# Tiles placed at equal addresses modulo 512 bytes, and the first MLP product as three 256-column matmuls

## The chip, the cores and the metric

The kernel runs on one core of one Trainium2 chip. The metric is the device time of one execution in microseconds, taken as the median of several runs. Nothing else runs on the chip.

## The reference

A trunk of four residual sub-layers over 256 tokens of width 2048, all in float32: a gated linear recurrence (RG-LRU), an MLP, dilated attention, and a second MLP, each behind an RMS norm, and a final norm.

```python
for i in range(2):
    h = _rmsnorm(x, mix_norm[i])
    x = x + (_rglru_block(h, ...) if i == 0 else _dilated_attention_block(h, ...))
    x = x + _mlp(_rmsnorm(x, mlp_norm[i]), mlp_w1[i], mlp_w2[i])
return _rmsnorm(x, final_norm)

def _mlp(h, w1, w2):                    # w1 2048 x 8192, w2 8192 x 2048
    u = jnp.einsum('bsd,df->bsf', h, w1)
    u = jnp.square(jax.nn.relu(u))
    return jnp.einsum('bsf,fd->bsd', u, w2)
```

The recurrent block projects to 2 x 2560 columns (`w_in`), runs a convolution, ten block-diagonal gates of width 256 and a scan, and projects back (`w_out`). The attention block projects to q, k and v (`w_qkv`) and back (`w_o`).

## The kernel before, in words

**Number format.** A float32 operand is cut into a high part, rounded to the matmul's float32r format, and a low part, the remainder. A product is the sum of three matmuls: high by high, high by low, low by high. ScalarE cuts the weights' high part `whi` (line 86), VectorE their low part `wlo` (line 90). A tokens' tile holds both parts side by side: columns 0 to 255 are the high part for 256 tokens, columns 256 to 511 the low part. The tokens' tiles are `xT0` to `xT3` (the normed input, four blocks of 128 features in each), `aT0` to `aT19` (a hidden activation, 128 features each) and `chl` (the gates' input).

**Units.** All weights stream in as units of up to 1 MiB (128 partitions by 2048 columns) in one fixed order, the order in which they are used. A unit is 16 blocks of 128 by 128, or 4 of 128 by 512. There are 3 raw buffers, 4 of `whi` and 3 of `wlo`, and loading and cutting run some units ahead. The order of all work is written out by hand: a list of items, one for each unit, with follow-up work hung on items behind (`after(n, ...)`).

**Three forms of product.** All their matmuls are issued from one line, 142.
- `stand_w`: a 128 x 128 block of weights is loaded into the array and 256 columns of a tokens' tile stream past. Three matmuls of 256 columns for each block. Used by the recurrent block's input projection (`acc<-xT,whi` and `acc<-xT,wlo` of 128x256), and written out in the same pattern in the gates (`g<-chl,...`).
- `stand_w2`: the same, but `whi` meets all 512 columns (high and low) in one matmul, which leaves two sums in a 512-column accumulator, and `wlo` meets the 256 high columns. One matmul of 512 and one of 256 for each block. Used by the first MLP product (`w1`): 64 units in each MLP.
- `stand_x`: a 128 x 128 block of tokens is loaded and 512 columns of weights stream past. 24 matmuls of 512 columns a unit. Used by q, k, v (`acc<-whi,xT`, `acc<-wlo,xT`), the output projections and the second MLP product (`acc<-whi,aT`, `acc<-wlo,aT`).

Every matmul has its own weight load (`PEld` in the profile), which the engine runs beside the matmul ahead.

**The first MLP product's end** is `u_done`: VectorE adds the two halves of the accumulator (line 462), multiplies the clipped sum by the norm's factor (line 463), ScalarE squares (465) and rounds (467), and VectorE takes the low part (471). Its result is `aT0` to `aT15`.

**Addresses.** Tiles are placed one behind the other within a partition, in the order in which a pool first meets their names. The byte at which they begin, modulo 512, as the built program has it:

| tile | before |
|---|---|
| raw, whi, wlo (all buffers) | 320 |
| aT0 to aT15 | 320 |
| xT0 to xT3 | 256 |
| chl, aT16 to aT19 | 352 |

A block's 128 columns are 512 bytes and a tokens' half 1024, so every operand that a matmul reads begins at the same place modulo 512 as its tile does. The tile `xb` (two rows of 259 floats, 2072 bytes) stands ahead of `chl` and `aT16` to `aT19` in its pool, and the small tile `rs` behind `xT3`. The accumulators, and the operands of the attention's own small matmuls, stay where they are throughout.

Of the kernel before, what the change touches and what calls it, by code (L numbers as in the profile page):

```python
# [10 lines left out]
F32 = mybir.dt.float32  # L11
F32R = mybir.dt.float32r
AF = mybir.ActivationFunctionType
OP = mybir.AluOpType
AX = mybir.AxisListType

D = 2048
S = 256
NT = S // 128
# [4 lines left out]
DFF = 8192  # L24
# [2 lines left out]
KR = DR // 128  # L27
NCH = D // 512
UW = 2048

PC = {}
_at = 0
# [17 lines left out]
def trunk(ctx: ExitStack, tc: tile.TileContext, a: dict, out: bass.AP):  # L50
    nc = tc.nc
    P = 128

    perm = ctx.enter_context(tc.tile_pool(name="perm", bufs=1))
# [1 line left out]
    psum = ctx.enter_context(tc.tile_pool(name="psum", bufs=1, space=bass.MemoryType.PSUM))  # L56
    ctx.enter_context(tc.manual_schedule())

    # ---- the order of the weights: units of up to 1 MiB, each with its columns a partition
    units = []  # L60

    def unit(ap, width=UW):
        units.append((ap, width))
        return len(units) - 1

    raw, split = {}, {}
    seen = {"load": 0, "hi": 0, "lo": 0}

    def load(i, step=UW):
        ap, width = units[i]  # L70
        r = wts.tile([P, UW], F32, name="raw", bufs=RAW_BUFS)
        raw[i] = []
        for at in range(0, width, step):
            s = slice(at, min(at + step, width))
            raw[i].append((s, r[:, s]))
            nc.sync.dma_start(r[:, s], ap[:, s])

    def new_hi(i):
        split[i] = (wts.tile([P, UW], F32R, name="whi", bufs=HI_BUFS),)

    def new_lo(i):
        split[i] += (wts.tile([P, UW], F32R, name="wlo", bufs=3),)

# [32 lines left out]
    def item(u, fn):  # L116
        items.append((u, fn))
# [18 lines left out]
    lru = Scope()  # L136

    def after(n, fn, *args):
        later.setdefault(now[0] + n, []).append((fn, args))

    def mm(o, l, r, start, stop):
        nc.tensor.matmul(o, l, r, start=start, stop=stop, skip_group_check=True)  # L142

    # ---- constants and small parameters
    par = perm.tile([P, NPAR], F32, name="par")
    con = perm.tile([P, NCON], F32, name="con")
    ident = con[:, 0:128]
# [1 line left out]
    def pcol(name, j):  # L149
        at = PC[name][0] + j  # L150
        return par[:, at:at + 1]

    xc = [perm.tile([P, NT, 512], F32, name=f"xc{n}") for n in range(NCH)]
    ssq = perm.tile([P, NT, NCH], F32, name="ssq", bufs=2)
    state = {}

    def hilo(hi_out, lo_out, src):
# [8 lines left out]
    def xT(k):  # L166
        return state["xT", k // 4][:, k % 4, :]
# [44 lines left out]
        nc.scalar.activation(rb, tr[:, 0, :], AF.Copy)  # L212
        state["rstdB"] = rb

    # ---- products of three parts: the weights' tile stands still, or the tokens' tile does
    def stand_w(ps, u, ks, w_at, first, last):
        hi, lo = split[u]
        for j, k in enumerate(ks):
            x = xT(k)
            s = slice((w_at + j) * 128, (w_at + j + 1) * 128)  # L220
            mm(ps, hi[:, s], x[:, 0:256], first and j == 0, False)
            mm(ps, hi[:, s], x[:, 256:512], False, False)
            mm(ps, lo[:, s], x[:, 0:256], False, last and j == len(ks) - 1)

    def stand_w2(ps, u, ks, w_at, first, last):
        hi, lo = split[u]
        for j, k in enumerate(ks):
            x = xT(k)
            s = slice((w_at + j) * 128, (w_at + j + 1) * 128)
            if first and j == 0:  # L230
                mm(ps, hi[:, s], x, True, False)
                mm(ps[:, 0:256], lo[:, s], x[:, 0:256], False, False)
            else:
                mm(ps[:, 0:256], lo[:, s], x[:, 0:256], False, False)
                mm(ps, hi[:, s], x, False, last and j == len(ks) - 1)

    def stand_x(acc, u, get, ks, first, last, ts=range(NT)):
        hi, lo = split[u]
# [9 lines left out]
    def acc_tile():  # L248
        return psum.tile([P, 512], F32, name="acc", bufs=4)

    accs = {}

    def out_item(key, u, get, ks, first, last, done):
        def run():
            if first:
                accs[key] = [acc_tile() for _ in range(NT)]
            stand_x(accs[key], u, get, ks, first, last)
            if last:
                after(0, done, accs.pop(key))
        item(u, run)  # L260
# [23 lines left out]
    def new_aT(j):  # L284
        t = (perm if j < 16 else lru).tile([P, 512], F32R, name=f"aT{j}")
        state["aT", j] = t
        return t

    # ---- the recurrent block
    spn = perm.tile([P, 2, KR], F32, name="spn")  # L290

    spw = perm.tile([P, 6, KR], F32, name="spw")
# [22 lines left out]
    blk = {}  # L315

    def xb_done(h, j, ps):
        if j == 0:
            blk[h, "xb"] = lru.tile([P, 2, S + 3], F32, name="xb")
            blk[h, "c"] = lru.tile([P, 2, S], F32, name="c", bufs=2)  # L320
            nc.vector.memset(blk[h, "xb"][:, :, 0:3], 0.0)
        xb, c, ch = blk[h, "xb"], blk[h, "c"], 2 * h + j
        nc.vector.tensor_mul(xb[:, j, 3:], ps[:, :S], state["rstdB"])
        nc.vector.tensor_scalar(c[:, j, :], xb[:, j, 3:], pcol("cw", 60 + ch), pcol("cb", ch),
                                op0=OP.mult, op1=OP.add)
        w = lru.tile([P, 2, S], F32, name="a") if h == 1 and j == 0 else None
        for i in range(3):
            if w is not None:
                nc.gpsimd.tensor_scalar(w[:, j, :], xb[:, j, i:i + S], pcol("cw", 20 * i + ch), None, op0=OP.mult)  # L329
                nc.gpsimd.tensor_add(c[:, j, :], c[:, j, :], w[:, j, :])  # L330
            else:
                nc.vector.scalar_tensor_tensor(c[:, j, :], xb[:, j, i:i + S], pcol("cw", 20 * i + ch),
                                               c[:, j, :], op0=OP.mult, op1=OP.add)
        if j == 1:
            after(1, conv_split, h)
# [120 lines left out]
            for kq in range(5):  # L456
                oproj(n, kq)

    # ---- the MLP, DFF in four parts
    def u_done(j, ps):  # L460
        r = lru.tile([P, S], F32, name="mr", bufs=2)
        nc.vector.tensor_reduce(r, ps.rearrange("p (b c) -> p c b", b=2), axis=AX.X, op=OP.add)  # L462
        nc.vector.scalar_tensor_tensor(r, r, 0.0, state["rstdB"], op0=OP.max, op1=OP.mult)  # L463
        uu = lru.tile([P, S], F32, name="mu", bufs=2)
        nc.scalar.activation(uu, r, AF.Square)  # L465
        t = new_aT(j)
        nc.scalar.activation(t[:, 0:256], uu, AF.Copy)  # L467
        after(1, u_low, t, uu)
# [4 lines left out]
    def plan_mlp(w1, w2, done):  # L473
        for c in range(4):
            us = []

            def part(j, ks, first, last, us=us, c=c):
                def run():
                    if first:
                        accs["u", j] = acc_tile()  # L480
                    stand_w2(accs["u", j], us[j], ks, ks[0], first, last)
                    if last:
                        after(1 if c == 0 and j == 0 else 0, u_done, j, accs.pop(("u", j)))
                item(us[j], run)

            us.extend(unit(w1[c * 16 + j]) for j in range(16))
            at = 0
            if c == 0:
                for j in range(2):
                    part(j, range(0, 12), True, False)  # L490
                for j in range(2):
                    part(j, range(12, 16), False, True)
                at = 2
            for j in range(at, 16):
                part(j, range(16), True, True)
            for n in range(NCH):
                last_c = c == 3
                if last_c and n == NCH - 1 and done is final_done:
                    final_items([unit(w2[(c * 4 + n) * 4 + kq]) for kq in range(4)])
                    continue  # L500
                for kq in range(4):
                    u = unit(w2[(c * 4 + n) * 4 + kq])
                    out_item(("m", n), u, aT, range(4 * kq, 4 * kq + 4), kq == 0, kq == 3,
                             done(n) if last_c else (lambda acc, n=n: add_x(n, acc)))

    # ---- dilated attention
    att = {}
    scale = HD ** -0.5

# [92 lines left out]
            for kq in range(4):  # L602
                oproj(n, kq)

    # ---- the end
    def final_done(n):
        def done(acc):
            if n == 0:
# [53 lines left out]
        nc.sync.dma_start(gB, a["g_fin"].to_broadcast([P, D]))  # L662
        state["gB"] = gB

    # ---- the plan
    first = [None] * 4
    lru.open("rec")
    plan_rec()
# [7 lines left out]
    item(None, load_g)  # L676
    plan_mlp(a["w1_1"], a["w2_1"], final_done)

    # ---- the start: the first units by the chunks of the tokens, as both arrive
    nc.sync.dma_start(par, a["par"])  # L680
    warm = perm.tile([P, 1], F32, name="warm")
    nc.vector.memset(warm, 0.0)
# [14 lines left out]
    for n in range(NCH):  # L697
        xg[n] = perm.tile([P, 4, S], F32, name="xg", bufs=2)
        rs = [wts.tile([P, UW], F32, name="raw", bufs=RAW_BUFS) for _ in range(3)] if n == 0 else rs
        for h in range(2 if n == 0 else 1):  # L700
            w = 2 if n == 0 else 4
            nc.sync.dma_start(xg[n][:, h * w:(h + 1) * w, :], a["xT"][:, 4 * n + h * w:4 * n + (h + 1) * w, :])
            for i in range(3):
                if n or i == 0:
                    s = slice(n * 512 + h * w * 128, n * 512 + (h + 1) * w * 128)
                elif h:
                    s = slice(0, 512)
# [5 lines left out]
        for h in range(2 if n == 0 else 1):  # L713
# [6 lines left out]
            for i in range(3):  # L720
# [3 lines left out]
                for at, (s, _) in enumerate(raw[i]):  # L724
                    if s.stop == n * 512 + (h + 1) * w * 128:
# [5 lines left out]
                        ks = range(s.start // 128, s.stop // 128)  # L731
# [14 lines left out]
    for n in range(NCH):  # L746
        s = slice(n * 512, (n + 1) * 512)
        r = xc[n // 2][:, n % 2, :]
# [14 lines left out]
    ps = psum.tile([P, 2, S], F32, name="tr", bufs=2)  # L763
# [102 lines left out]
```

## Time and profile before

| | us |
|---|---|
| runs | 2205.47, 2207.06, 2207.97 |
| median | 2207.06 |
| span of the profiled execution, first to last instruction | 2202.6 |
| TensorE busy with matmuls, in that span | 2179.4 |
| VectorE, ScalarE, GpSimd busy | 1315.3, 1062.0, 80.1 |
| HBM traffic | 411 MB, 187 GB/s over the span |

The profile gives the profiled execution's span; its whole time is not listed apart from the three runs. The median stands 4.5 us above the span, for what lies ahead of the first instruction and behind the last. TensorE's busy share counts overlapping instructions once, and the ends of matmuls are modelled, so the pace of a stream of matmuls is read from their starts. The program's stages by time: start to 43 us, recurrent input projection with gates to 276, `w_out` to 382, first MLP to 1095 (four rounds of 16 units of `w1` and 16 of `w2`), attention to 1484, second MLP to the end.

### The profile page before, as it was taken

How to read it: one execution, taken by the hardware profiler on the slowest of the kernel's cores; microseconds unless marked ns; L12 is line 12 of the kernel's file. 1: busy time of each engine (PE TensorE's matmuls, PEld its weight loads, DVE VectorE, ACT ScalarE, POOL GpSimd, SP SyncE). 2: the span in 40 equal slices, each digit the busy share in tenths (PEclk: the TensorE clock that was granted, in tenths of full speed). 3: DMA queues.
4: the chain of work that ended last, by engine and by line, in shares of the span. 5: the costliest groups of instructions: out<-in, count | busy, mean ns of one | idle time of the engine just before them, and what ended most of it. 6: DMA issues, size and time to landing. Idle time of an engine off the chain costs nothing.

```text
span 2202.6 us, 27925 instructions
## 1 busy us (share of the span) xinstructions
PE 2179.4 (99%) x11722; PEld 1877.8 (85%) x11722; DVE 1315.3 (60%) x1392; ACT 1062.0 (48%) x1163; POOL 80.1 (4%) x42
## 2 busy tenths in 40 slices
PE   7999999999999999999999999999999999999998
PEld 7999988888888888888888888888888888888886
DVE  8899855654564564565455555456545645645654
ACT  5787755543443443344445445455434434433442
POOL 2221100000000000000000000000000000000001
PEclk9999999999999999999999999999999999999999
DMA  6666555555555555555554455455555555555553
GB/s 222 207 211 205 197 191 191 180 196 196 176 192 197 184 190 193 189 191 191 182 191 162 163 177 177 162 199 183 195 196 177 191 196 184 190 193 190 191 191 115
DMA packets 61694, 413.30 MB, mean 188 GB/s; under 512 B 6784, under 2 KB 7168, under 8 KB 13440
## 3 DMA queue, kind: packets, MB, share of 16 engines
q1 hardware_dynamic: 61568, 411.51, 54.7%
q8 instruction: 92, 1.51, 0.3%
q14 instruction: 34, 0.28, 0.0%
HBM read 409.39 MB, written 2.10 MB: 187 GB/s over the span
## 4 chain that ended last, share of the span: by engine, by line
PE 96%; DVE 2%; ACT 1%; POOL 0%; issue 0%; DMA 0%; SPq 0%; DVEq 0%; ACTq 0%
PE acc L142 93%; PE g L142 1%; DVE wlo L90 1%; PE tr L176 0%; DVE xT L718 0%; PE tr L537 0%; PE g L545 0%; PE tr L568 0%; POOL a L329 0%; DMA raw<-in_w_in 0%; POOL c L330 0%; PE g L578 0%; PE g L577 0%; PE g L576 0%; PE g L544 0%
## 5 line engine op out<-in xcount | busy, mean ns | idle before, releaser
L90 DVE TENSOR_TENSOR wlo<-raw,whi 128x2048 fp32r<-128x2048 f32 (+3 forms) x400 | 885.5, 2218 | 343.6 <-PE acc L142 267.4
L86 ACT ACTIVATE whi<-raw 128x2048 fp32r<-128x2048 f32 (+3 forms) x400 | 737.1, 1844 | 519.7 <-PE acc L142 398.6
L142 PE MATMUL acc<-xT,whi 128*128 128x512 f32 (+1 forms) x3296 | 935.0, 353 | 6.5 <-ACT whi L86 6.0
L142 PE MATMUL acc<-whi,aT 128*128 128x512 f32 x2624 | 814.0, 390 | 0.0
L142 PE MATMUL acc<-xT,wlo 128*128 128x256 f32 x2672 | 729.8, 281 | 8.2 <-DVE wlo L90 8.1
L142 PEld LDWEIGHTS acc<-xT,whi 128*128 128x128 f32 x3296 | 569.5, 189 | 89.7 <-ACT whi L86 6.3
L142 PEld LDWEIGHTS acc<-whi,aT 128*128 128x128 f32 x2624 | 492.6, 188 | 102.0
L142 PEld LDWEIGHTS acc<-xT,wlo 128*128 128x128 f32 x2672 | 503.9, 189 | 21.3 <-DVE wlo L90 9.3
L142 PE MATMUL acc<-wlo,aT 128*128 128x512 f32 x1312 | 510.7, 389 | 0.0
L142 PEld LDWEIGHTS acc<-wlo,aT 128*128 128x128 f32 x1312 | 246.4, 188 | 50.9
L142 PE MATMUL acc<-whi,xT 128*128 128x512 f32 x768 | 245.9, 396 | 0.0
L465 ACT ACTIVATE mu<-mr 128x256 f32<-128x256 f32 x128 | 53.5, 418 | 378.6 <-DVE mr L463 378.4
L462 DVE TENSOR_REDUCE mr<-acc 128x256 f32<-128x512 f32 x128 | 88.5, 691 | 242.8 <-PE acc L142 242.7
L142 PEld LDWEIGHTS acc<-whi,xT 128*128 128x128 f32 x768 | 144.3, 188 | 30.7
L142 PE MATMUL acc<-wlo,xT 128*128 128x512 f32 x384 | 150.4, 392 | 0.0
L264 DVE TENSOR_TENSOR xc<-xc,acc 128x512 f32<-128x512 f32 x78 | 53.2, 687 | 98.1 <-PE acc L142 98.0
L142 PEld LDWEIGHTS acc<-wlo,xT 128*128 128x128 f32 x384 | 72.2, 188 | 15.1
L612 POOL TENSOR_TENSOR xc<-xc,gB 128x1024 f32<-128x1024 f32 x3 | 10.6, 3519 | 1886.5 <-DMA raw<-in_w 1850.0
L463 DVE SCALAR_TENSOR_TENSOR mr<-mr,rstdB 128x256 f32<-128x256 f32 x128 | 54.4, 425 | 4.5
L467 ACT ACTIVATE aT<-mu 128x256 fp32r<-128x256 f32 x128 | 53.6, 419 | 4.1
L471 DVE TENSOR_TENSOR aT<-mu,aT 128x256 fp32r<-128x256 f32 x128 | 53.3, 418 | 0.0
L159 DVE TENSOR_TENSOR xT<-xg,xT 128x512 fp32r<-128x512 f32 x24 | 15.5, 689 | 54.0 <-ACT xT L158 54.0
(142 smaller groups left out, 765.7 us busy)
## 6 DMA issues: line engine op xcount, KB each, us to landing
raw<-in_w SPq DMA_DIRECT2D x256, 1024.0 KB, 4.8
raw<-in_w_qkv SPq DMA_DIRECT2D x48, 1024.0 KB, 4.8
raw<-in_w_in SPq DMA_DIRECT2D x35, 1024.0 KB, 4.9
raw<-in_w_out SPq DMA_DIRECT2D x20, 1024.0 KB, 4.9
raw<-in_w_o SPq DMA_DIRECT2D x16, 1024.0 KB, 4.8
raw<-in_w_g SPq DMA_DIRECT2D x10, 512.0 KB, 3.5
raw<-in_w_in SPq DMA_DIRECT2D x11, 256.0 KB, 6.3
xc<-in_x SPq DMA_DIRECT2D x4, 512.0 KB, 6.1
```

The source lines that it names most:

```text
L86: nc.scalar.activation(split[i][0][:, s], r, AF.Copy)
L90: nc.vector.tensor_sub(split[i][1][:, s], r, split[i][0][:, s].bitcast(F32))
L142: nc.tensor.matmul(o, l, r, start=start, stop=stop, skip_group_check=True)
L159: nc.vector.tensor_sub(lo_out, src, hi_out.bitcast(F32))
L264: nc.vector.tensor_add(xc[n][:, t, :], xc[n][:, t, :], acc[t])
L462: nc.vector.tensor_reduce(r, ps.rearrange("p (b c) -> p c b", b=2), axis=AX.X, op=OP.add)
L463: nc.vector.scalar_tensor_tensor(r, r, 0.0, state["rstdB"], op0=OP.max, op1=OP.mult)
L465: nc.scalar.activation(uu, r, AF.Square)
L467: nc.scalar.activation(t[:, 0:256], uu, AF.Copy)
L471: nc.vector.tensor_sub(t[:, 256:512], uu, t[:, 0:256].bitcast(F32))
L612: nc.gpsimd.tensor_mul(xc[n], xc[n], state["gB"][:, None, n * 512:(n + 1) * 512].to_broadcast([P, NT, 512]))
```

## The change

Three edits. The first MLP product goes through `stand_w` (three matmuls of 256 columns into one 256-column sum) in place of `stand_w2`, so `u_done` has nothing to add up and reads the accumulator directly. A first `rs` tile is asked for right behind `ssq`, which moves that name ahead of everything after it and `xT` 64 bytes on. `xb` gets rows of 320 floats in place of 259, so that it takes 2560 bytes, and only columns 0 to 258 are used.

```diff
+XBW = 320
...
     ssq = perm.tile([P, NT, NCH], F32, name="ssq", bufs=2)
+    perm.tile([P, 4, NT], F32, name="rs", bufs=2)
...
-    def stand_w2(ps, u, ks, w_at, first, last):
-        hi, lo = split[u]
-        for j, k in enumerate(ks):
-            x = xT(k)
-            s = slice((w_at + j) * 128, (w_at + j + 1) * 128)
-            if first and j == 0:
-                mm(ps, hi[:, s], x, True, False)
-                mm(ps[:, 0:256], lo[:, s], x[:, 0:256], False, False)
-            else:
-                mm(ps[:, 0:256], lo[:, s], x[:, 0:256], False, False)
-                mm(ps, hi[:, s], x, False, last and j == len(ks) - 1)
...
-            blk[h, "xb"] = lru.tile([P, 2, S + 3], F32, name="xb")
+            blk[h, "xb"] = lru.tile([P, 2, XBW], F32, name="xb")
...
-        nc.vector.tensor_mul(xb[:, j, 3:], ps[:, :S], state["rstdB"])
-        nc.vector.tensor_scalar(c[:, j, :], xb[:, j, 3:], pcol("cw", 60 + ch), pcol("cb", ch),
+        nc.vector.tensor_mul(xb[:, j, 3:3 + S], ps[:, :S], state["rstdB"])
+        nc.vector.tensor_scalar(c[:, j, :], xb[:, j, 3:3 + S], pcol("cw", 60 + ch), pcol("cb", ch),
...
-        nc.vector.tensor_reduce(r, ps.rearrange("p (b c) -> p c b", b=2), axis=AX.X, op=OP.add)
-        nc.vector.scalar_tensor_tensor(r, r, 0.0, state["rstdB"], op0=OP.max, op1=OP.mult)
+        nc.vector.scalar_tensor_tensor(r, ps[:, :S], 0.0, state["rstdB"], op0=OP.max, op1=OP.mult)
...
-                    stand_w2(accs["u", j], us[j], ks, ks[0], first, last)
+                    stand_w(accs["u", j][:, :S], us[j], ks, ks[0], first, last)
```

The addresses modulo 512 after it: `xT0` to `xT3` 320, `chl` and `aT16` to `aT19` 320, and raw, `whi`, `wlo` and `aT0` to `aT15` 320 as before. So each pair of operands of a float32r matmul begins at the same place modulo 512.

TensorE's queue in the first MLP, where one unit of `w1` ends and the next begins (a row is one instruction or a run of equal ones; names are out<-moving operand, stationary operand, with buffer numbers). Before:

```order
L142 MATMUL acc_4104<-xT3_4014,wlo_3972 128x256
L142 MATMUL acc_4104<-xT3_4014,whi_3934 128x512
L142 MATMUL acc_4152<-xT0_3601,whi_3970 128x512
L142 MATMUL acc_4152<-xT0_3601,wlo_4036 128x256 x2
L142 MATMUL acc_4152<-xT0_3601,whi_3970 128x512
```

The same place after:

```order
L143 MATMUL acc_4135<-xT3_4027,whi_3935 128x256 x2
L143 MATMUL acc_4135<-xT3_4027,wlo_3973 128x256
L143 MATMUL acc_4198<-xT0_3602,whi_3971 128x256 x2
L143 MATMUL acc_4198<-xT0_3602,wlo_4049 128x256
L143 MATMUL acc_4198<-xT0_3602,whi_3971 128x256 x2
```

Each matmul of 512 columns has become two of 256, and the low product stands last in every group of three. Every other row of TensorE's queue is as before.

VectorE's queue in the same stage, at the ends of two units (`mr` is `u_done`'s working tile). Before:

```order
L462 TENSOR_REDUCE mr_4280<-acc_4246 128x256
L463 SCALAR_TENSOR_TENSOR mr_4280<-mr_4280,rstdB_4082 128x256
L90 TENSOR_TENSOR wlo_4291<-raw_4146,whi_4242 128x2048
L471 TENSOR_TENSOR aT5_4285<-mu_4283,aT5_4285 128x256
L462 TENSOR_REDUCE mr_4327<-acc_4293 128x256
```

After:

```order
L452 SCALAR_TENSOR_TENSOR mr_4372<-acc_4322,rstdB_4115 128x256
L91 TENSOR_TENSOR wlo_4382<-raw_4192,whi_4318 128x2048
L460 TENSOR_TENSOR aT5_4376<-mu_4374,aT5_4376 128x256
L452 SCALAR_TENSOR_TENSOR mr_4434<-acc_4384,rstdB_4115 128x256
```

The reduction is gone, one for each unit of `w1`, and nothing else moved. The rows of ScalarE, GpSimd and the DMA queue are the same in both.

## The prediction

> **What bounds the kernel now.** I read the page first: engines, clock and the chain that ended last.
>
> ```profile
> PE 2179.4 (99%) x11722; PEld 1877.8 (85%) x11722; DVE 1315.3 (60%) x1392; ACT 1062.0 (48%) x1163; POOL 80.1 (4%) x42
> PEclk9999999999999999999999999999999999999999
> PE 96%; DVE 2%; ACT 1%; POOL 0%; issue 0%; DMA 0%; SPq 0%; DVEq 0%; ACTq 0%
> ```
>
> TensorE never rests and runs at full clock, and 96% of the chain is its own work. So the time changes only if the stream of matmuls gets shorter, or if somebody else starts to hold it up. The groups of instructions by form say what the stream is made of (count | busy us, mean ns of one).
>
> ```profile
> L142 PE MATMUL acc<-whi,aT 128*128 128x512 f32 x2624 | 814.0, 390 | 0.0
> L142 PE MATMUL acc<-xT,whi 128*128 128x512 f32 x2048 | 715.2, 397 | 0.0
> L142 PE MATMUL acc<-wlo,aT 128*128 128x512 f32 x1312 | 510.7, 389 | 0.0
> L142 PE MATMUL acc<-whi,xT 128*128 128x512 f32 x768 | 245.9, 396 | 0.0
> L142 PE MATMUL acc<-wlo,xT 128*128 128x512 f32 x384 | 150.4, 392 | 0.0
> L142 PE MATMUL g<-chl,whi 128*128 128x256 f32 x160 | 28.5, 279 | 0.0
> ```
>
> Matmuls of the same 512 columns do not last equally long: 390 ns with `aT`, 396 or 397 with `xT`. A mean duration holds the time through the array, so the pace has to be read from starts. The timeline of TensorE gives them (start us, us, operation). Five stretches, each by its first and last row:
>
> ```profile
> 420.07 0.28 PE L142 MATMUL acc<-xT,wlo 128*128 128x256 f32 x1
> 420.19 0.40 PE L142 MATMUL acc<-xT,whi 128*128 128x512 f32 x1
> ...
> 448.27 0.28 PE L142 MATMUL acc<-xT,wlo 128*128 128x256 f32 x1
> ...
> 501.79 0.39 PE L142 MATMUL acc<-wlo,aT 128*128 128x512 f32 x1
> ...
> 537.83 0.39 PE L142 MATMUL acc<-wlo,aT 128*128 128x512 f32 x1
> ...
> 1110.20 0.39 PE L142 MATMUL acc<-wlo,xT 128*128 128x512 f32 x1
> ...
> 1136.30 0.39 PE L142 MATMUL acc<-wlo,xT 128*128 128x512 f32 x1
> ...
> 318.81 0.40 PE L142 MATMUL acc<-wlo,aT 128*128 128x512 f32 x1
> ...
> 324.41 0.40 PE L142 MATMUL acc<-wlo,aT 128*128 128x512 f32 x1
> ...
> 57.73 0.28 PE L142 MATMUL acc<-xT,wlo 128*128 128x256 f32 x1
> ...
> 70.10 0.28 PE L142 MATMUL acc<-xT,wlo 128*128 128x256 f32 x1
> ```
>
> - First MLP product (`stand_w2`, moving operand at 256, stationary at 320): 28.20 us for 80 pairs, 352.5 ns a pair.
> - Second MLP product with `aT0` to `aT15` (both at 320): 36.04 us for 159 matmuls, 226.7 ns each.
> - q, k, v (moving 320, stationary 256): 26.10 us for 114, 228.9 ns each.
> - The recurrent output projection with `aT16` to `aT19` (moving 320, stationary 352): 5.60 us for 24, 233.3 ns each. This is the same line and form as the second stretch, with only the address changed.
> - An early unit of the recurrent input projection (`stand_w`, moving 256, stationary 320): 12.37 us for 105, 117.8 ns each.
>
> The same projection goes faster later. The chain in order of time is unbroken there (start us, us, what):
>
> ```profile
> 84.31 16.39 PE acc L142 x142
> 103.49 21.95 PE acc L142 x192
> 125.44 2.80 PE g L142 x24
> 128.24 21.78 PE acc L142 x192
> 251.14 21.79 PE acc L142 x168
> ```
>
> 128.24 to 150.02 holds 192 matmuls, 113.4 ns each, half of 226.7: the best pace that any float32r matmul here keeps. The gate at 125.44 (moving 352, stationary 320) takes 2.80 us for 24, 116.7 ns. So equal addresses always go at the best pace, unequal ones at 1 to 4% above it, except that the projection, at 64 bytes apart, has both paces.
>
> **The change part by part.**
>
> *The first MLP product.* 2048 pairs at 352.5 ns become 2048 groups of three 256-column matmuls. The trace has no `stand_w` at equal addresses. Its nearest rows are the late projection (113.4, same form, 64 bytes apart) and the early one (117.8, the same). I take 113.4, since the only streams at equal addresses keep exactly twice that for 512 columns: 3 x 113.4 = 340.2, 12.3 ns less, 2048 x 12.3 = 25.2 us gained. At 117.8 a group takes 353.4, and 1.8 us are lost. I find no row with a shorter pace for this form, so the gain ends there.
>
> A split matmul could also carry a fixed cost. The rows say no: two at 113.4 are 226.8, one of 512 is 226.7. The Trainium skill, page "TensorE: Matmul & The Clock Gate", section "Back-to-back issue gap", puts the warm gap at N / 2.4 + 2.5 ns, and so charges 2.5 ns for each further matmul. By that rule 2048 more of them would cost an estimated 5.1 us against the wide form, and the stage would not gain at all. This trace does not bear it out.
>
> *q, k, v.* 768 + 384 = 1152 matmuls from 228.9 to 226.7, since they become the form and the offset of the `aT` stream: 2.5 us. Ends: 0 if the address does nothing, and 2.8 where the slower intervals between the attention's small matmuls count too.
>
> *Gates.* 240 matmuls (the 160 with `whi`, and 80 with `wlo`) from 116.7 to 113.4: 0.8 us; ends 0.8 and, at 117.8, a loss of 0.3.
>
> *`aT16` to `aT19`.* One unit in each of four column chunks, 4 x 24 x (233.3 - 226.7) = 0.6 us, or 0.
>
> *The projection.* Late units already go at 113.4, so 0; at 117.8 it would be a loss, priced below. The early units could gain about 250 x 4.4 ns = 1.1 us between 45 and 75 us. I book 0: the chain there does not run through TensorE but through GpSimd and the cutting of weights, and it ends at a late `wlo`.
>
> ```profile
> 59.17 3.10 POOL a L329
> 81.97 2.29 DVE wlo L90
> ```
>
> *VectorE.* 128 reductions go, and the multiply reads the accumulator instead of `mr`.
>
> ```profile
> L462 DVE TENSOR_REDUCE mr<-acc 128x256 f32<-128x512 f32 x128 | 88.5, 691 | 242.8 <-PE acc L142 242.7
> L463 DVE SCALAR_TENSOR_TENSOR mr<-mr,rstdB 128x256 f32<-128x256 f32 x128 | 54.4, 425 | 4.5
> L323 DVE TENSOR_TENSOR xb<-acc,rstdB x19: 409/416/425, 42.9 to 256.6; 128x256 f32<-128x256 f32 x19
> ```
>
> A 256-column operation on an accumulator takes 416 ns where one from a tile takes 425, so 88.5 us of VectorE work vanish. On the path that is 0: the reduction sat idle 242.7 us waiting for TensorE, and its result is wanted a round later.
>
> *Cover.* A faster first product needs a unit every 5.44 us (48 x 113.4) in place of 5.64 (16 x 352.5). The recurrent stage already lives at that pace with a busier VectorE, as the busy time by stretch shows (PE, PEld, DVE, ACT, POOL with counts, clock, DMA share, GB/s; the recurrent stage, then the MLP):
>
> ```profile
> 82.00:276.00 194.00, 191.74 (x1657) 190.62 (x1657) 175.90 (x223) 151.66 (x184) 39.18 (x16) 1.00 0.62 207
> 562.00:650.00 88.00, 88.00 (x501) 76.49 (x500) 56.62 (x61) 40.52 (x46) 0.00 (x0) 1.00 0.54 180
> ```
>
> VectorE is 91% busy in the first and 64% in the second, and the DMA moves 207 GB/s there. What is late next would be the cut of the weights; all its waits on TensorE are small:
>
> ```profile
> PE acc L142 <- DVE wlo L90: 8.1, 4, 2.7
> PE acc L142 <- ACT whi L86: 6.0, 2, 5.7
> ```
>
> They sit in the start and the early recurrence, where the change adds no work. If that cover were gone, each unit would wait up to one cut, 2.2 us; I see no reason for it.
>
> *Sum.* 25.2 + 2.5 + 0.8 + 0.6 = 29.1 us. The span 2202.6 becomes 2173.5, and with the 4.5 us by which the median stands above the span, 2178.0.
>
> **The rivals.**
>
> *The slow pace catches the whole of `stand_w`* (slower). The early projection shows that this form can lock to 117.8 ns for some 30 us, with the operands of the late one, so something besides the offset decides, perhaps where the weight load and the moving stream stand against each other. For it: in this form the loads run almost without a break (190.62 of 194 us, against 76.49 of 88 in the MLP), and no row shows it at offset 0. Against it: every stream at offset 0 keeps the best pace, straight after any interruption. Price: at a pace p the whole changes by 2048 x (352.5 - 3p) - 1462 x (p - 113.4) ns, plus 3.9 us from the other three terms, where 1462 = 142 + 6 x 192 + 168 are the late projection's matmuls in the chain. That is zero at p = 117.2. At 117.8 the kernel is 4.4 us slower: 2211.5.
>
> *It falls back and forth* between the paces, mean 115.6: the same formula gives 12.4 us gained, 2194.7.
>
> *The addresses do nothing* and the paces belong to forms: then only the 25.2 us of the first product come, 2181.9. Against it stands the pair 226.7 and 233.3, one form at two offsets. The Trainium skill, page "SBUF — State Buffer", section "A bandwidth-pool intuition that's wrong (but worth ruling out)", speaks for this rival: it gives TensorE an independent second read port for weight loads and knows only structural contention, in which an operand's address plays no part. The pair disagrees with it.
>
> **How the numbers follow.** The forecast: 0.70, within 2174 to 2182. Addresses do nothing: 0.08. Back and forth, anywhere from 2183 to 2205: 0.12. Slow throughout, 2206 to 2214: 0.08. Better than the sum, below 2172, by a pace that no row shows: 0.02. The range 2172 to 2196 holds the first two and some two thirds of the third. A measurement tells 0.2%, 4.4 us, from no change: faster is below 2202.6, and takes the first three but a little and the last, 0.90; the slow case sits on the upper edge, 2211.5, and is shared, 0.05 same and 0.05 slower.
>
> **What would show it.** 13770 matmuls, no reduction, VectorE near 1227 us busy. In the MLP three starts per 340 ns. q, k, v at 226.7, gates 2.72 us for 24, no early stretch at 117.8. Wrong would be starts 118 ns apart in the first product or in the late projection, or new waits for `wlo` in the MLP.

## The result, and the profile after

The changed kernel takes 2227.2 us (median of four runs, 2224.5 to 2228.22), against 2206.26 us for the kernel before (its three runs above and a fourth, 2204.4 to 2207.97). The ratio is 1.0095, 95% interval 1.0082 to 1.0109: 0.95% slower. Forecast were 2178.0 us and a range that ended at 2196. The profiled execution spans 2224.8 us, 22.2 more than before, at the same granted clock (0.998).

The page of the changed kernel: busy time of the engines, clock by slices, and the chain by engine.

```profile
PE 2200.7 (99%) x13770; PEld 1996.3 (90%) x13770; DVE 1223.3 (55%) x1264; ACT 1060.8 (48%) x1163; POOL 77.0 (3%) x42
PEclk9999999999999999999999999999999999999999
PE 96%; DVE 2%; ACT 1%; POOL 0%; DMA 0%; issue 0%; DVEq 0%; SPq 0%; ACTq 0%
```

The bound is where it was: the chain runs through TensorE for 96%, and TensorE is busy 21.3 us longer. VectorE lost 92.0 us, where the forecast had 88.5, and nothing came of it. The waits of TensorE exclude that somebody holds it up (who is waited for: us in total, times, longest):

```profile
PE acc L143 <- DVE wlo L91: 8.1, 5, 2.5
PE acc L143 <- ACT whi L87: 6.3, 1, 6.3
PE acc L143 <- DVE xT L707: 0.8, 1, 0.8
```

These 15.2 us, 14.6 before, all lie in the first 100 us, in both kernels. So the stream of matmuls itself became longer. The chain in order of time says where (start us, us, piece). Of the kernel before, the two pieces that hold nearly all of the two MLPs:

```profile
394.87 638.11 PE acc L142 x3256
1496.22 697.95 PE acc L142 x3520
```

Of the kernel after, two pieces of the recurrent projection and the same two of the MLPs:

```profile
129.57 23.04 PE acc L143 x192
259.17 22.75 PE acc L143 x168
403.46 645.54 PE acc L143 x4248
1510.52 705.38 PE acc L143 x4512
```

Each MLP became 7.43 us longer, not 12.6 shorter; a piece of the projection takes 23.04 us where it took 21.78. The pace behind this is read from starts in TensorE's timeline (first and last row of four stretches: first MLP product, late projection with gates, q, k, v, and the output projection with `aT16` to `aT19`):

```profile
420.10 0.28 PE L143 MATMUL acc<-xT,wlo 128*128 128x256 f32 x1
...
448.18 0.28 PE L143 MATMUL acc<-xT,wlo 128*128 128x256 f32 x1
...
130.36 0.28 PE L143 MATMUL acc<-xT,wlo 128*128 128x256 f32 x1
...
150.16 0.28 PE L143 MATMUL acc<-xT,wlo 128*128 128x256 f32 x1
...
1117.93 0.40 PE L143 MATMUL acc<-wlo,xT 128*128 128x512 f32 x1
...
1149.90 0.39 PE L143 MATMUL acc<-wlo,xT 128*128 128x512 f32 x1
...
328.40 0.39 PE L143 MATMUL acc<-wlo,aT 128*128 128x512 f32 x1
...
333.16 0.39 PE L143 MATMUL acc<-wlo,aT 128*128 128x512 f32 x1
```

- First MLP product: 28.08 us for 234 matmuls, 120.0 ns each, 360.0 a block, where the pair took 352.5.
- Late projection: 19.80 us for 165, 120.0 ns each, where it kept 113.4.
- q, k, v: 31.97 us for 141, 226.7 ns each, as forecast.
- `aT16` to `aT19`: 4.76 us for 21, 226.7 ns each, as forecast.

The groups of instructions by form carry the same in their means, since a matmul's recorded duration here is its pace plus some 163 ns, 284 against 120.0 and 390 against 226.7 (count | busy us, mean ns of one):

```profile
L143 PE MATMUL acc<-xT,whi 128*128 128x256 f32 x5344 | 966.0, 284 | 7.1 <-ACT whi L87 6.3 <-DVE xT L707 0.8
L143 PE MATMUL acc<-whi,aT 128*128 128x512 f32 x2624 | 813.7, 390 | 0.0
L143 PE MATMUL acc<-xT,wlo 128*128 128x256 f32 x2672 | 757.6, 284 | 8.1 <-DVE wlo L91 8.1
L143 PE MATMUL acc<-whi,xT 128*128 128x512 f32 x768 | 244.7, 394 | 0.0
L143 PE MATMUL g<-chl,whi 128*128 128x256 f32 x160 | 29.2, 283 | 0.0
```

Every `stand_w` matmul, gates included, has 283 or 284 ns, that is 120.0. The account of the 22.2 us: the MLPs' pieces +14.9; the late projection 1462 x (120.0 - 113.4) = +9.6; the gates 240 x (120.0 - 116.7) = +0.8; q, k, v 1152 x (226.7 - 228.9) = -2.5; `aT16` to `aT19` -0.6. Together 22.2. That it closes to the tenth is partly luck. By the starts of the pieces, the way to the first MLP's piece grew by 8.6 us, where the terms ahead of it give 9.8, the stretch between the two MLPs' pieces shrank by 1.7, where q, k, v give 2.5, and 0.5 were added behind the last one.

From 226.7 to 120.0 ns is 106.7 ns for 256 columns. So, read as a fixed charge for each matmul, the two forms carry 13.3 ns beside their columns at equal places, whatever the width, and splitting one matmul into two would pay it twice. This reading sets moving tokens against moving weights, and `e1_addresses` below goes against it. The charge is of the kind that the Trainium skill, page "TensorE: Matmul & The Clock Gate", section "Back-to-back issue gap", puts at 2.5 ns and that the forecast set aside. Read so, it would be five times that here.

### The profile page after: what moved, and what is told of

The parts are those of the page before. It is cut to its first block, busy times and chain, and to the rows that moved or that the text cites. A ratio compares the mean times of both kernels' runs of the same rounds, so it can differ in the third digit from the quotient of the medians.

```text
span 2224.8 us, 32015 instructions
## 1 busy us (share of the span) xinstructions
PE 2200.7 (99%) x13770; PEld 1996.3 (90%) x13770; DVE 1223.3 (55%) x1264; ACT 1060.8 (48%) x1163; POOL 77.0 (3%) x42
## 4 chain that ended last, share of the span: by engine, by line
PE 96%; DVE 2%; ACT 1%; POOL 0%; DMA 0%; issue 0%; DVEq 0%; SPq 0%; ACTq 0%
PE acc L143 93%; PE g L143 1%; DVE wlo L91 1%; PE tr L178 0%; DMA xg<-in_xT 0%; DVE xT L707 0%; PE tr L526 0%; PE g L534 0%; PE tr L557 0%; POOL a L319 0%; POOL c L320 0%; PE g L567 0%; PE g L566 0%; PE g L565 0%; PE g L533 0%
## 5 line engine op out<-in xcount | busy, mean ns | idle before, releaser
L143 PE MATMUL acc<-xT,whi 128*128 128x256 f32 x5344 | 966.0, 284 | 7.1 <-ACT whi L87 6.3
L143 PEld LDWEIGHTS acc<-xT,whi 128*128 128x128 f32 x5344 | 836.0, 192 | 8.1 <-ACT whi L87 6.3
L143 PE MATMUL acc<-xT,wlo 128*128 128x256 f32 x2672 | 757.6, 284 | 8.1 <-DVE wlo L91 8.1
L143 PEld LDWEIGHTS acc<-xT,wlo 128*128 128x128 f32 x2672 | 513.8, 192 | 9.2 <-DVE wlo L91 9.2
L452 DVE SCALAR_TENSOR_TENSOR mr<-acc,rstdB 128x256 f32<-128x256 f32 x128 | 54.2, 425 | 345.0 <-PE acc L143 345.0
L191 ACT ACTIVATE junk<-xc 128x512 bf16<-128x512 f32 x32 | 20.2, 632 | 55.9 <-DVE xc L254 37.4
```

Source lines behind the costliest of these rows:

```text
L191: nc.scalar.activation(junk, xc[n][:, t, :], AF.Square, accum_out=sq[:, t, n:n + 1])
L452: nc.vector.scalar_tensor_tensor(r, ps[:, :S], 0.0, state["rstdB"], op0=OP.max, op1=OP.mult)
```

## The experiments

The expectations name theories by letters. O: the distance between where the moving and the stationary operand begin sets the pace. F: the form sets it (three narrow matmuls cost it, wherever the tiles lie). B: other engines' or transfers' accesses to the same memory do. H: what ran on TensorE just before does. S: at some distances there are two stable paces, and the entry into the stream picks one. R: what the bare measurement shows does not carry over, or the pace falls by chance. W: weights come late. C: the move of `chl`, `aT16` to `aT19`, not that of `xT`, did it. Here "distance" is where the tokens' tile begins minus where the weights do, whichever of the two moves; so the old `xT` lies at -64, that is 192 modulo 256, and the old gates and `aT16` to `aT19` at 32.

**One half each.** `e1_addresses` is the kernel before with only the tiles moved; the first MLP product keeps `stand_w2`.

```diff
+    perm.tile([P, 4, NT], F32, name="rs", bufs=2)
...
-            blk[h, "xb"] = lru.tile([P, 2, S + 3], F32, name="xb")
+            blk[h, "xb"] = lru.tile([P, 2, XBW], F32, name="xb")
```

> The addresses of the change alone (all operands of the float32r matmuls at 320 modulo 512), with the first MLP product still in its wide form (one matmul of 512 columns and one of 256 for each block). Theory O (offset): the pace of a matmul is its columns at full clock (106.7 ns for 256, 213.3 for 512) plus a stall from the weight load that runs beside it, and the stall depends on where the two operands begin modulo 512. At equal places it is 13.3 ns for either width, as the changed kernel's 120.0 and 226.7 suggest. Then the recurrent projection goes at 120.0 ns here too, the gates at 120.0, q, k, v at 226.7, and a pair of the first MLP product at 226.7 + 120.0 = 346.7 in place of 352.5: about 9.6 us lost in the projection, 0.8 in the gates, 2.5 and 0.6 gained in q, k, v and aT16 to aT19, 11.9 gained in the MLP, near 2203. Theory F (form): the three narrow matmuls in the MLP are what slows the kernel, and the projection's 120.0 is their after-effect. Then the projection keeps 113.4 here, the MLP pair 352.5, and the time is near 2203 too; the paces tell the two apart.

Measured: 2213.03 us, ratio 1.0036 (1.0023 to 1.0049). Its chain, a piece of the projection and the two of the MLPs:

```profile
129.30 23.04 PE acc L143 x192
402.98 638.34 PE acc L143 x3256
1502.62 698.18 PE acc L143 x3520
```

The addresses alone make the projection as slow as in the changed kernel (23.04 us, 120.0 ns), with the old form of the MLP. The MLPs stay where they were (638.34 against 638.11): the pair takes 353.1 ns from start to start, 235.8 and 117.3, where it took 352.5, and not the 346.7 of 226.7 and 120.0. So a charge of 13.3 ns for each matmul does not hold for `stand_w2`, and O missed it.

`e2_three` is the kernel before with only the form changed; all tiles stay, `xT` at 256 and the weights at 320.

```diff
-        nc.vector.tensor_reduce(r, ps.rearrange("p (b c) -> p c b", b=2), axis=AX.X, op=OP.add)
-        nc.vector.scalar_tensor_tensor(r, r, 0.0, state["rstdB"], op0=OP.max, op1=OP.mult)
+        nc.vector.scalar_tensor_tensor(r, ps[:, :S], 0.0, state["rstdB"], op0=OP.max, op1=OP.mult)
...
-                    stand_w2(accs["u", j], us[j], ks, ks[0], first, last)
+                    stand_w(accs["u", j][:, :S], us[j], ks, ks[0], first, last)
```

> The three matmuls of 256 columns in the first MLP product alone, with all addresses as before (tokens at 256, weights at 320 modulo 512). Theory O: the pace is that of the recurrent projection at these addresses, 113.4 or 117.8 ns: a block takes 340 or 353 ns, and the kernel 2182 or 2209 us. Theory F: 120.0 ns as in the changed kernel, 360 ns a block, 15 us slower, near 2222.

Measured: 2204.84 us, ratio 0.9997 (0.9987 to 1.0006), no change. In TensorE's timeline, first and last row of a stretch in the second round of `w1`, then of one in the first round of the second MLP:

```profile
571.26 0.28 PE L142 MATMUL acc<-xT,wlo 128*128 128x256 f32 x1
...
640.16 0.28 PE L142 MATMUL acc<-xT,wlo 128*128 128x256 f32 x1
...
1505.10 0.28 PE L142 MATMUL acc<-xT,wlo 128*128 128x256 f32 x1
...
1560.18 0.28 PE L142 MATMUL acc<-xT,wlo 128*128 128x256 f32 x1
```

68.90 us for 585 matmuls is 117.8 ns; 55.08 us for 486 is 113.3. One kernel, one line, the same tiles, two paces. Of the eight rounds of `w1`, seven run at 117.8, and one, the first of the second MLP, at 113.3 behind its first 96 matmuls. Those go at the slow pace, and the norm's transposes break the stream between them and the rest. So 120.0 belongs to the new addresses (F falls), and at the old ones the form has two paces. At 113.3 in all rounds the split would have brought about what was forecast.

**Other distances, in the whole kernel.** Two variants of the changed kernel spread the tiles by padding, with one run each. `e3_scan` puts the four `xT` 288 to 480 bytes from the weights' place and the `aT` at sixteen distances; `e4_scan` puts the `xT` at 64 to 192 and all `aT` at the weights' place. Both keep one buffer fewer for the norm's factor, to make room.

```diff
-        t = perm.tile([P, 4, 512], F32R, name=f"xT{n}")
+        t = perm.tile([P, 4, 512], F32R, name="xT" + "abcd"[n])
+        if ("xT", n) not in state and XPAD[n]:
+            perm.tile([P, XPAD[n] // 4], F32, name="padx" + "abcd"[n])
```

> The changed kernel with the four tokens' tiles of the normed input at four different distances from the weights (tokens minus weights, modulo 512 bytes: xTa 288, xTb 352, xTc 416, xTd 480) and the sixteen tiles aTa to aTp at sixteen (weights minus tokens: 480, 448 and so on down to 0, in steps of 32). The norm factor's tile has one buffer in place of two, to make room. Theory O: within one unit the pace steps from tile to tile, 256 columns anywhere between 107 and 120 ns, 512 columns between 213 and 235, and 13.3 above the floor where the distance is 0. Theory F: 120.0 with every xT tile, 226.7 with every aT tile.

> The same with other distances for the normed input: tokens minus weights 64 (xTa), 96 (xTb), 160 (xTc), 192 (xTd), and all aT tiles at the weights' place as before. Theory O: four paces within one unit, the second MLP product at 226.7 throughout. Theory F: 120.0 with every xT tile.

Measured: 2244.46 and 2222.33 us. By tile, from start to start within a tile in the first MLP, `stand_w` goes at 117.5, 120.0, 118.5 and 118.5 ns (distances 288, 352, 416, 480), and at 118.0, 119.5, 118.2 and 117.1 (64, 96, 160, 192). No distance is better than 117, but each unit passes through four of them, so each is entered from another. The groups of two `aT` tiles in `e3_scan`, at distances 256 apart, and of one in `e4_scan`:

```profile
L145 PE MATMUL acc<-whi,aTp 128*128 128x512 f32 x160 | 56.9, 395 | 0.0
L145 PE MATMUL acc<-whi,aTh 128*128 128x512 f32 x160 | 57.0, 396 | 0.0
```

```profile
L145 PE MATMUL acc<-whi,aTp 128*128 128x512 f32 x160 | 55.9, 389 | 0.0
```

`aTp` lies at the weights' place in both kernels. Among neighbours at other distances it takes 395 ns (231.0 from start to start), among its like 389 (226.7). The neighbours matter, which speaks for H and S.

**The paces by themselves.** `e5_paces` leaves the rest of the computation out: one unit of weights and sixteen tokens' tiles 32 bytes apart, and nothing but matmuls on TensorE, in streams of one distance each, behind a known stream. Two of its five sections, in the kernel's text:

```python
    # 1: three narrow ones, behind a wide stream at equal places
    for n in ORDER:
        stand_x(xs[0])
        for _ in range(3):
            stand_w(xs[n])
    # 2: the same, behind narrow ones at 32
    for n in ORDER:
        stand_w(xs[1], 8)
        for _ in range(3):
            stand_w(xs[n])
```

> A measurement of the paces by themselves: one unit of weights, cut once, and sixteen copies xa to xp of one tokens' tile, each 32 bytes further from the weights' place (tokens minus weights 0, 32, ... 480 modulo 512). No other engine works and no DMA runs while TensorE goes through five sections: three narrow matmuls a block with each tile, behind a wide stream at equal places; the same behind narrow ones at 32; the wide form (512 and 256); weights moving past the tokens' tile; and the narrow ones again behind a pause. The rest of the computation is left out. Theory O (the distance of the two operands sets the pace, TensorE alone makes the stall): narrow matmuls at 0 go at 120.0 ns, weights moving at 0 at 226.7, distances 256 apart behave alike, and 192 and 448 (the place before) show 113.3 or 117.8. Rival B (the stalls come from the other engines' and the DMA's use of the memory): here every stream goes at one pace, near 107 to 109 ns for 256 columns and 213 to 216 for 512, at every distance. Rival H (history): at one distance the pace differs between the sections.

The kernel took 1607.63 us, which has nothing to be compared with. Mean ns from start to start, by distance; distances 256 apart gave the same within 0.2 ns. Behind a pause, where TensorE waited for a ScalarE copy ahead of each stream, it is the mean of the last two thirds of a stream:

| distance modulo 256 | 0 | 32 | 64 | 96 | 128 | 160 | 192 | 224 |
|---|---|---|---|---|---|---|---|---|
| `stand_w` behind a wide stream | 120.0 | 116.7 | 117.8 | 120.0 | 120.0 | 118.7 | 117.8 | 118.3 |
| `stand_w` behind a narrow one at 32 | 120.0 | 116.7 | 117.8 | 120.0 | 118.7 | 118.7 | 113.4 | 118.3 |
| `stand_w` behind a pause | 120.0 | 117.8 | 117.8 | 120.0 | 118.7 | 117.3 | 113.3 | 118.3 |
| `stand_w2`, a pair | 352.9 | 348.0 | 351.7 | 350.1 | 350.8 | 347.7 | 352.5 | 352.7 |
| `stand_x`, weights moving | 226.7 | 233.4 | 233.3 | 234.2 | 232.4 | 233.4 | 229.0 | 233.3 |

First and last row of four stretches in its timeline: the tile at distance 0, then the one at 192 behind a wide stream, then the same one behind a narrow stream, then the one at 32 behind a pause.

```profile
19.82 0.28 PE L53 MATMUL accd<-xa,wlo 128*128 128x256 f32 x1
...
34.22 0.28 PE L53 MATMUL accb<-xa,wlo 128*128 128x256 f32 x1
...
155.06 0.28 PE L53 MATMUL accb<-xo,wlo 128*128 128x256 f32 x1
...
169.55 0.28 PE L53 MATMUL accd<-xo,wlo 128*128 128x256 f32 x1
...
497.03 0.28 PE L53 MATMUL accc<-xo,wlo 128*128 128x256 f32 x1
...
510.97 0.28 PE L53 MATMUL acca<-xo,wlo 128*128 128x256 f32 x1
...
1409.99 0.28 PE L53 MATMUL accc<-xj,wlo 128*128 128x256 f32 x1
...
1420.24 0.28 PE L53 MATMUL accd<-xj,wlo 128*128 128x256 f32 x1
```

14.40 us for 120 is 120.0 ns; 14.49 for 123 is 117.8; 13.94 for 123 is 113.3; 10.25 for 87 is 117.8. The paces of the whole kernels come back within a tenth of a nanosecond with no other engine at work: 120.0 and 226.7 at 0, 116.7 and 233.4 at 32 (the old gates, and the old `aT16` to `aT19`), and at 192 (the old `xT`) 352.5, 117.8, 113.4 and 229.0. That ends B. It also settles what "distance" means: the weights begin at 128 modulo 512 in this program and at 320 in the whole kernel, so tokens at 64 modulo 256 go at 120.0 in the changed kernel and at 113.4 or 117.8 here. The place relative to the weights decides, not the address by itself.

`stand_w` and `stand_x` have opposite tastes: distance 0 is the best place for moving weights and, with 96, the worst for moving tokens. And H holds beside O: the entry changes the pace at 32, 128 and 160 too, not only at 192. At 0, 64, 96 and 224 all three entries gave one pace. The Trainium skill, page "SBUF — State Buffer", section "A bandwidth-pool intuition that's wrong (but worth ruling out)", gives TensorE a second independent read port for weight loads; if the two ports were independent in every respect, no row of this table should depend on the distance, and every one does.

`e6_entries` leaves the rest out too. It asks what picks the pace at 192: a wide stream at distance 0, then one of thirteen entries, then 96 narrow matmuls at 192, and the entries in three different orders. `Y` is a tile at 32, `X` the one at 192, and the last two numbers give the columns.

```python
    ENTRIES = [
        lambda: None,
        lambda: narrow(Y, 1),
        lambda: narrow(Y, 3),
        lambda: narrow(Y, 24),
        lambda: narrow(X, 1, 0, 128),
        lambda: narrow(X, 1, 0, 64),
        lambda: narrow(X, 1, 0, 16),
        ...
```

> What picks the pace at the place before (192 modulo 256). The same bare measurement: a wide stream of weights at equal places (24 matmuls), an entry, then 96 narrow matmuls with the tile at 192. Thirteen entries, each three times in three orders: nothing; 1, 3 or 24 narrow matmuls with the tile at 32; one matmul of 128, 64 or 16 columns with the tile itself; one or two of 512; two narrow ones with the tile at 0; the first two narrow ones in another order; one plain float32 matmul; a pause for a ScalarE copy. The rest of the computation is left out. Theory S (two stable states, chosen at the entry): nothing gives 117.8 ns for all 96, the 24 narrow ones at 32 and the pause give 113.3, as in the run before, each entry gives the same state all three times, and no stream changes its pace in the middle. Rival R (chance): the same entry gives different paces in its three turns, or a stream changes by itself.

First and last row of the 94 last narrow matmuls behind no entry, then of those behind one matmul of 64 columns:

```profile
241.44 0.28 PE L53 MATMUL accd<-xg,wlo 128*128 128x256 f32 x1
...
252.40 0.28 PE L53 MATMUL acca<-xg,wlo 128*128 128x256 f32 x1
...
258.30 0.28 PE L53 MATMUL acca<-xg,wlo 128*128 128x256 f32 x1
...
268.86 0.28 PE L53 MATMUL accb<-xg,wlo 128*128 128x256 f32 x1
```

10.96 us for 93 is 117.8 ns; 10.56 us for 93 is 113.5, with the entry's own delay in it, and 113.3 after it. Each entry gave the same pace in all three orders, and no stream changed its pace on the way. 117.8 came behind nothing, one or 24 narrow ones at 32, one of 128 or 16 columns, and two more at 192 with the low product first; 113.3 behind three narrow ones at 32, one of 64 columns, one or two of 512, two narrow ones at 0, and one plain float32 matmul. That 24 narrow ones gave the slow pace is a miss of S as expected: in `e5_paces` 24 at 32 led to 113.4, but those went through both parts of the weights and these through the high part alone. The entry meant as a pause made none, since the ScalarE copy in it had an old input, and gave what no entry gives. So the two paces are stable and the entry decides, but no simple rule of the entry is visible.

**The entry, in the whole kernel.** `e7_entry64` is `e2_three` with a matmul of 64 columns, whose result is overwritten, ahead of the first unit of each later round of `w1`, and ahead of the fourth unit in the first round. `e8_entry512` has 512 columns in its place.

```diff
                         accs["u", j] = acc_tile()
+                        if j == (3 if c == 0 else 0):
+                            mm(accs["u", j][:, :64], split[us[j]][0][:, 0:128], xT(0)[:, 0:64], True, True)
```

> The addresses of before, three narrow matmuls in the first MLP product, and a throwaway matmul of 64 columns ahead of one unit in each of the eight rounds of w1 (ahead of the first unit, or of the fourth where a round follows the norm's transposes); its result is overwritten. Theory S (two stable states at this distance, chosen at the entry, kept until the stream ends): the rounds behind it go at 113.3 ns in place of 117.8, 16 x 48 x 4.4 ns = 3.4 us a round; seven rounds, since one of the eight was fast without it, give 23.9 us less 8 x 0.14, so about 2182. The two rounds behind the norm are less sure, since their entry is another stream: 2185 if one stays slow. Rival R (the entry works only where nothing else runs): 117.8, 2205. Rival W (the faster stream runs into late weights): 113.3 ns, but new waits for the cutting of weights that eat the gain.

> The same with one throwaway matmul of 512 columns in place of the 64. Theory S: the same paces, and 8 x 0.2 us for the throwaways, about 2183. It differs from the other where a round is already fast when the throwaway comes. Rival R: 2205.

Measured: 2185.46 us, ratio 0.991 (0.9894 to 0.9927), and 2185.02 us, ratio 0.9909 (0.9895 to 0.9924). The two pieces of the MLPs in the chain of `e7_entry64`:

```profile
395.90 626.44 PE acc L142 x4252
1485.62 688.86 PE acc L142 x4516
```

And of its timeline, the first and last row of a stretch in the first round of the second MLP, behind the entry:

```profile
1499.74 0.28 PE L142 MATMUL acc<-xT,wlo 128*128 128x256 f32 x1
...
1560.16 0.28 PE L142 MATMUL acc<-xT,wlo 128*128 128x256 f32 x1
```

One instruction a round takes 12.4 us from the first MLP of `e2_three` (638.84 there, without it) and 6.9 from the second (695.73). Seven rounds now run at 113.3 behind their entries. The eighth, the first of the second MLP, ran at 113.3 without the entry, and still does ahead of it; behind it 60.42 us for 513 matmuls is 117.8. So the entry doesn't lead to the good pace, it shifts a stream that is on the wrong one, and also one that is on the right one. An entry of 64 columns and one of 512 do the same, as they did by themselves. TensorE's waits for the cutting of weights did not grow (13.4 us, 15.1 in `e2_three`), so W falls. So S holds, though not as a cure that always helps.

Chance is not wholly out, though. The recurrent projection up to 130 us is the same in the kernel before, `e2_three`, `e7_entry64` and `e8_entry512`, in instructions and addresses. Yet the 192 matmuls that start at 103 to 105 us went at 117.8 throughout in `e8_entry512`, and at 113.3 but for the first few in `e2_three` and `e7_entry64`, though the same 24 matmuls of the gates came just before in all three. What differs in the traces is a wait for weights some 20 us earlier, 2.52 us there and 2.69 in the other two. So more than the last few matmuls can count, perhaps their timing; no run tests that.

**Which move, and the best of both.** `e9_xt_back` takes from the changed kernel the early `rs` tile, so `xT` goes back to 256 while `chl` and `aT16` to `aT19` stay moved. `e10_best` adds the entry of 64 columns to it, in the later rounds alone.

```diff
-    perm.tile([P, 4, NT], F32, name="rs", bufs=2)
```

> The changed kernel with one edit undone, the early rs tile: xT is back at 256, 192 from the weights modulo 256, and chl and aT16 to aT19 stay at the weights' place. Theory O/S (the move of xT onto the weights' place is what slows the changed kernel): no narrow matmul with xT at 120.0 ns any more, the first MLP product at 117.8 or 113.3, gates at 120.0, and the whole near the kernel before: 2205, or 2211 if the projection takes the slow state behind its gates. Rival C (the move of chl, aT16 to aT19 does it): 2227 as the changed kernel.

```diff
                         accs["u", j] = acc_tile()
+                        if c and j == 0:
+                            mm(accs["u", j][:, :64], split[us[j]][0][:, 0:128], xT(0)[:, 0:64], True, True)
```

> The version the runs point to: the changed kernel with xT back at 256, and the throwaway matmul of 64 columns only ahead of the second, third and fourth round of w1 in each MLP (the first rounds were fast without it in the run with xT back). Theory S: all eight rounds and the projection at 113.3 ns; 2200.6 less 6 x 3.4 plus 6 x 0.14, about 2181, faster than both kernels and than the two runs with an entry in every round. Rival: the first rounds fall to 117.8 again, 2188.

Measured: `e9_xt_back` 2200.64 us, ratio 0.9978 (0.9969 to 0.9987); `e10_best` 2181.25 us, ratio 0.9887 (0.987 to 0.9903). The MLPs' pieces in the chain of the first, then of the second:

```profile
394.71 635.88 PE acc L143 x4248
1493.85 695.73 PE acc L143 x4512
```

```profile
395.91 626.10 PE acc L143 x4251
1485.27 685.95 PE acc L143 x4515
```

With `xT` back nothing that it feeds runs at 120.0: the first rounds of both MLPs run at 113.3 behind their first 96 matmuls, the later six at 117.8. The gates, still moved, stay near 120 (119.2 in the mean). So `xT`'s 64 bytes cost some 26 us (ratios 1.0095 and 0.9978), and C falls. The entry then takes 9.78 us from each MLP, 3.26 a round, and all eight rounds are near 113.4. This version beats both kernels, by 24.8 us the one before and by some 46 the changed one, and stands 3 us from the time that was forecast for the change.

## Why the prediction was wrong

- **The step that failed** is the pace of `stand_w` at equal addresses. It took 113.4 ns, half of what 512 moving columns take there. The runs show 120.0, in the changed kernel, with the addresses alone, and by itself. The argument carried a pace from moving weights at distance 0 to moving tokens at distance 0, and the two forms differ there; the prediction had noted itself that no row showed this form at equal addresses. Each of the 2048 groups was to take 340.2 ns in place of 352.5 and took 360.0. The term meant as a gain of 25.2 us was a loss, 14.9 us of it in the two pieces of the MLPs.
- **The projection, booked at nothing**, lost 9.6 us by its paces (9.3 by its pieces in the chain) by the same step: it had been at the one place with a pace of 113.4 and was moved from it. The forecast wrote that unequal places always go slower, except for this; the exception was the rule that mattered.
- **The claim that a split carries no fixed cost** compared moving tokens at distance 192 (113.4) with moving weights at distance 0 (226.7). With tokens moving and the distance 0, three narrow ones take 360.0 ns where the pair takes 353.1, so there the split costs 6.9; at 192 it gains 12.3 or loses 0.9, by the pace that the narrow ones fall into.
- **The gates** were given a gain of 0.8 us and cost 0.8 (24 take 2.88 us, not 2.72), again the same step.
- **Right:** q, k, v and `aT16` to `aT19` at 226.7, with 3.1 us gained together by these paces; 13770 matmuls; VectorE at 1223 us (forecast 1227) with nothing on the path; no new wait for `wlo`.
- **The 4.5 us between span and median**, the last term of the sum, are not what lies outside the span: the changed kernel's profiled execution took 2226.55 us with a span of 2224.8, which leaves 1.8. By that the kernel before, with its span of 2202.6, took about 2204.4 when it was profiled, which is less than its median. The forecast does not suffer, since the gain was taken from the median all the same.
- **The rivals.** "The slow pace catches the whole of `stand_w`" came nearest, at a chance of 0.08: all of `stand_w` did run slow. With 120.0 for its p its formula gives 21.1 us slower, and 20.9 were measured, with some luck, since it counts the gates as a gain. But its pace, 117.8, was that of another address, and its reason, a pace that the form falls into, is not what acts at distance 0, where all three entries of `e5_paces` gave 120.0. Its guess that something beside the distance decides at 192 is shown by `e6_entries` and `e7_entry64`. "Back and forth" did not happen: in the changed kernel `stand_w` stays at 120.0 wherever it does not wait. "The addresses do nothing" is excluded by `e1_addresses` and `e5_paces`, and "better than the sum" by the result.

What stays open: why there are two paces, and why distance 0 suits one form and not the other. In the trace's records nearly every weight load begins 2 to 4 ns after the start of the matmul ahead of it, so load and moving stream run through memory side by side, and a collision that depends on their distance would fit. No run here shows such a collision.

## What to carry to other kernels

Take the pace of a stream from a row with the same form, the same width and the same distance between moving and stationary operand; where no row has all three, the price is unknown, and a range that rests on a neighbour must reach to the far row. When one line of a profile shows two paces for one form at one address, find out what chooses between them before changing sizes or places: here one throwaway matmul ahead of a round was worth 3.3 us a round, while the intended change lost 21. And a change made of two parts is judged in parts: the split alone did nothing (`e2_three`), the addresses alone lost 7.4 us (`e1_addresses`), and the split with `xT` left in place is the base of the best version.

## What was not expected of the hardware

- With float32r operands the pace of back-to-back matmuls depends on the distance between moving and stationary operand modulo 256 bytes, measured in steps of 32: 113.3 to 120.0 ns for 256 columns, 226.7 to 234.2 for 512 columns of weights, 347.7 to 352.9 for a pair of both widths.
- At some distances there are two paces for one form, and what ran just before picks one: 113.3 and 117.8 ns at 192, 116.7 and 117.8 at 32, 118.7 and 120.0 at 128, 117.3 and 118.7 at 160. At 192 they hold for hundreds of matmuls, each of thirteen entries gave the same one all three times, and a single matmul of 64 columns switches between them.
- Neither needs another engine: `e5_paces` and `e6_entries` show them with TensorE alone, and the mean clock granted was 0.996 to 0.999 of full in all runs.
